# Plain products for the first 512 inner features of each MLP, PSUM banks kept through all stages, pools re-ordered

## The chip, the cores and the metric

The kernel runs on one core of a Trainium2 chip. The metric is the device time of one execution in microseconds (us). The kernel before was timed three times: 2895.0, 2896.69 and 2899.65 us; the median, 2896.69 us, is the time that the change is compared with.

## The reference

One sequence of 1024 tokens with 1024 features goes through an HGRN2 mixer, a squared-ReLU MLP, a multi-head latent attention (MLA) with its shared keys and values, a second MLP and a final norm, all in float32. What the change touches is the MLP and the norms around it:

```python
def rmsnorm(x, gain):
    y = x * lax.rsqrt(jnp.mean(x * x, axis=-1, keepdims=True) + EPS)
    return y * gain

def sq_relu_mlp(xn, w_up, w_down):           # (1024,1024) @ (1024,4096), (4096,1024)
    return jnp.square(jax.nn.relu(xn @ w_up)) @ w_down

h = x
h = h + hgrn2_mixer(rmsnorm(h, hgrn_norm[0]), ...)
h = h + sq_relu_mlp(rmsnorm(h, mlp_norm[0]), mlp_w_up[0], mlp_w_down[0])      # MLP 0
k_nope, k_rope, v = shared_mla_kv(h, kv_in_norm, ...)
h = h + mla_mixer(rmsnorm(h, mla_norm[0]), ..., k_nope, k_rope, v)
h = h + sq_relu_mlp(rmsnorm(h, mlp_norm[1]), mlp_w_up[1], mlp_w_down[1])      # MLP 1
out = rmsnorm(h, final_norm)
```

## The kernel before

The residual stream stays on chip as `hT`, features on partitions, in two halves of 512 tokens (u = 0, 1); the program's rows call it `res`. Every float32 product is done in three matmuls: each operand is split into a high part (a cast to fp32r, on ScalarE, `wh`, `xn`, `hh`) and a low part (the difference, on VectorE or GpSimd, `wl`, `xn`, `hl`), and high x high, high x low and low x high are added in PSUM. A matmul has 512 columns.

**Stages.** HGRN2 mixer (to about 672 us of the profile), MLP 0 (to 1372), MLA (to 2187), MLP 1 (to the end). Each stage opens its own pools of on-chip memory and of PSUM banks: one bank `nb` and three banks `mm` in a mixer, eight banks `ps` in an MLP.

**An MLP** handles its 4096 inner features in eight blocks of 512. A block goes up (two calls of `up`, each for 256 inner features) and down (one call of `down`). Both use the Strassen-Winograd scheme: the operands are cut in 2x2 quarters, and seven products of sums stand for the eight products of quarters. The four quarters of the normed input are B11, B21 (token half 0; the two halves of the 1024 features) and B12, B22 (token half 1). The scheme also needs the sums T1 to T4, made once per MLP on VectorE (`combine` and the low part in `halves`, L529) and ScalarE (the cast in `halves`, L572), in 128x1024 pieces; the 4096-column buffers `fr` and `dn` hold the normed input meanwhile, and later the inner features and the weights of the way down. A product is 12 matmuls (L612); an `up` has 7, so 84 matmuls, a block's two 168, and its `down` (L745) 168.

**The start of an MLP** is `up_first`: both calls of the first block together, product by product. It starts with `inverse(0)` (squares, their sum over features, a matmul with ones (L557), logarithm and exponential, one Newton step) and `normed` (L566) for token half 0, then the products with B11 and B21; the others need T1 to T4, and so both halves of the tokens, `inverse(1)` too. In MLP 1, `finish.turn` also transposes the residual on TensorE (L1159) while the products run.

**The order on the engines** is that of a scheduler which follows the order of the program and its priorities: within `tc.high_priority(offset=n)` an instruction is placed as if it stood n instructions earlier. Each engine works off its own instructions in that fixed order, and waits at each for what it needs.

**In `up`**, the first product's bank x is copied to `fr` by ScalarE (L691) before the third product adds onto x; ScalarE also casts the weights (L602) and the hidden features of the way down (L730). **In `down`** each group of four banks collects 128-row pieces of the output, and VectorE adds them to the residual (L752). In the last block GpSimd also scales and splits the first weights of the next stage (L136, L145, L146, L879 to L882), and the MLA's start splits the residual (L100 on ScalarE, L101 on VectorE) and takes its norm (L484, L486). The scratch of the last `down` lies in the slot `xl0` of a pool for the whole kernel.

Of the kernel before, what the change touches and what calls it, by code (L numbers as in the profile page):

```python
# [17 lines left out]
P = 128  # L18
# [37 lines left out]
def build(nc, tc, a):  # L56
# [8 lines left out]
    pers = ctx.enter_context(tc.tile_pool(name="pers", bufs=1))  # L65
    cur = {}

    @contextmanager
    def common(stage):

        with tc.tile_pool(name=f"w_{stage}", bufs=1, reuse_waits="tile") as w, \
                tc.tile_pool(name=f"n_{stage}", bufs=1, reuse_waits="tile") as n, \
                tc.tile_pool(name=f"o_{stage}", bufs=1, reuse_waits="tile") as o, \
                tc.tile_pool(name=f"one_{stage}", bufs=1, space=PSUM, reuse_waits="tile") as one, \
                tc.tile_pool(name=f"b_{stage}", bufs=1, space=PSUM, reuse_waits="tile") as b:
            cur.update(w=w, n=n, o=o, one=one, b=b)
            yield
            cur.clear()
# [74 lines left out]
    def nbank():  # L153
        return cur["one"].tile([P, 512], F32, tag="nb", name=name("nb"), bufs=1)

    def bank():
        return cur["b"].tile([P, 512], F32, tag="mm", name=name("mm"), bufs=3)
# [347 lines left out]
    def mlp(layer, gain, finish):  # L505
# [5 lines left out]
        with ExitStack() as pools:  # L511
            mt, mu, mw, mf, mh, mp = (pools.enter_context(tc.tile_pool(name=f"mlp{n}{layer}", bufs=1,
                                                                       reuse_waits="tile")) for n in "tuwfhp")
# [23 lines left out]
            for key in ("T2", "T3", "T4"):  # L537
                X[key] = tuple(mt.tile([P, 4, 512], F32R, name=f"{key}{e}") for e in "hl")
            fr = mf.tile([P, 4096], F32, name="fr")
            dn = mf.tile([P, 4096], F32, name="dn")  # L540
            f = {}
            for i, t in enumerate((fr, dn)):
                v = t.rearrange("p (q k t) -> p q k t", q=2, k=4)
                f[i, 0], f[i, 1] = v[:, 0], v[:, 1]
# [4 lines left out]
            def inverse(u):  # L549
# [6 lines left out]
                ps = pbank()  # L556
# [33 lines left out]
            with tc.high_priority(offset=1000):  # L590
# [5 lines left out]
                if finish is not None:  # L596
                    finish.turn(0, pbank)
# [25 lines left out]
            def up_first(A, C):  # L623

                two = range(2)
                w = [parts(G, A[e][0, 0]) for e in two]
                x = [pbank() for _ in two]
                for e in two:
                    product(x[e], w[e], "B11", True, True)
                w = [parts(G, A[e][0, 1]) for e in two]  # L630
                y = [pbank() for _ in two]
                for e in two:
                    product(y[e], w[e], "B21", True, True)
                inverse(1)
                normed(0, 1)
                combine(V, f[0, 1], f[0, 1], f[0, 0])
                halves(V, "T1", f[0, 1])
                normed(1, 1)
                if finish is not None:
                    finish.turn(1, pbank)  # L640
                halves(V, "B22", f[1, 1])
                for e in two:
                    sub(G, A[e][1, 0], A[e][1, 0], A[e][1, 1], ALU.add)
                w = [parts(G, A[e][1, 0]) for e in two]
                z = [pbank() for _ in two]
                for e in two:
                    product(z[e], w[e], "T1", True, True)
                combine(V, f[1, 1], f[1, 1], f[0, 1])
                combine(V, f[0, 1], f[1, 1], f[0, 0])
                halves(V, "T2", f[1, 1])  # L650
                halves(V, "T3", f[0, 1])
                for e in two:
                    sub(G, A[e][1, 0], A[e][1, 0], A[e][0, 0])
                    sub(G, A[e][0, 1], A[e][0, 1], A[e][1, 0])
# [593 lines left out]
```

## Time and profile before

| what | value |
|---|---|
| median of three runs | 2896.69 us |
| the profiled execution's own time | 2896.47 us |
| its span in the trace | 2894.7 us |
| TensorE busy | 2674.8 us (92%), 13141 matmuls |
| VectorE, ScalarE, GpSimd busy | 1850.2, 1195.3, 1348.8 us |
| mean granted TensorE clock | 0.969 of full |

The profiled execution is within 0.3 us of the median, and 1.8 us of it lie outside the span. [...] In the timeline a row is one instruction or a run of like ones: its start, its duration, engine, source line, operation, out<-in, sizes, the count, and in brackets how long the engine had been idle and for what it waited. Matmuls overlap, so a single one's duration is longer than the step from one to the next.

### The profile page before, as it was taken

How to read it: one execution, taken by the hardware profiler on the slowest of the kernel's cores; microseconds unless marked ns; L12 is line 12 of the kernel's file. 1: busy time of each engine (PE TensorE's matmuls, PEld its weight loads, DVE VectorE, ACT ScalarE, POOL GpSimd, SP SyncE). 2: the span in 40 equal slices, each digit the busy share in tenths (PEclk: the TensorE clock that was granted, in tenths of full speed). 3: DMA queues.
4: the chain of work that ended last, by engine and by line, in shares of the span. 5: the costliest groups of instructions: out<-in, count | busy, mean ns of one | idle time of the engine just before them, and what ended most of it. 6: DMA issues, size and time to landing. Idle time of an engine off the chain costs nothing.

```text
span 2894.7 us, 35239 instructions
## 1 busy us (share of the span) xinstructions
PE 2674.8 (92%) x13141; PEld 2200.6 (76%) x13141; DVE 1850.2 (64%) x2970; ACT 1195.3 (41%) x2232; POOL 1348.8 (47%) x870
## 2 busy tenths in 40 slices
PE   7999999896899999996989999999996999999997
PEld 5777877785677787785778888888884777877785
DVE  6677667755855555557676666667667755555567
ACT  4222233223444444444354444444443544444445
POOL 3222223353677766767221122122212777767675
PEclk9999999997999999998999999999997899999999
DMA  4111112140211111110111111111100111111111
GB/s 130 40 37 30 30 44 59 52 135 19 66 52 52 51 59 51 59 55 24 53 42 34 28 50 40 36 39 35 48 19 26 58 52 51 59 51 59 59 48 58
DMA packets 184489, 143.99 MB, mean 50 GB/s; under 512 B 12482, under 2 KB 155903, under 8 KB 184319
## 3 DMA queue, kind: packets, MB, share of 16 engines
q1 hardware_dynamic: 184318, 141.75, 16.3%
q8 instruction: 103, 1.69, 0.2%
q14 instruction: 68, 0.55, 0.1%
HBM read 133.33 MB, written 4.19 MB: 48 GB/s over the span
## 4 chain that ended last, share of the span: by engine, by line
PE 67%; DVE 17%; POOL 6%; ACT 6%; issue 2%; DMA 1%; SPq 0%; DVEq 0%; POOLq 0%; ACTq 0%
PE mm L108 21%; PE ps L612 16%; PE ps L745 13%; PE s L1044 5%; PE nb L1077 3%; DVE hl L529 3%; POOL wl L529 2%; PE mm L1084 2%; POOL wu L529 2%; PE x L366 2%; DVE fr L529 2%; DVE res L752 1%; POOL dn L529 1%; ACT wh L602 1%; ACT hh L730 1%
## 5 line engine op out<-in xcount | busy, mean ns | idle before, releaser
L108 PE MATMUL mm<-xn,wh 128*128 128x512 f32 x1728 | 568.5, 403 | 1.5 <-DVE res L445 0.6
L529 POOL TENSOR_TENSOR wl<-dn,wh 128x512 fp32r<-128x512 f32 x224 | 342.1, 1537 | 115.7 <-ACT wh L602 104.0
L108 PEld LDWEIGHTS mm<-xn,wh 128*128 128x128 f32 x1728 | 321.5, 190 | 64.9 <-issue 3.0
L108 PE MATMUL mm<-xn,wl 128*128 128x512 f32 x864 | 347.2, 402 | 0.0
L146 POOL TENSOR_TENSOR wl<-wst,wh 128x1024 fp32r<-128x1024 f32 (+1 forms) x93 | 221.1, 2380 | 242.9 <-ACT wh L143 240.2
L529 POOL TENSOR_TENSOR wl<-wu,wh 128x512 fp32r<-128x512 f32 x156 | 216.5, 1393 | 186.1 <-PE ps L612 110.5
L752 DVE TENSOR_TENSOR res<-res,ps 128x512 f32<-128x512 f32 x448 | 289.6, 681 | 16.1 <-PE ps L745 15.0
L612 PE MATMUL ps<-xn,wh 128*128 128x512 f32 x1024 | 262.5, 399 | 25.2 <-ACT xn L572 16.2
L602 ACT CAST wh<-dn 128x512 fp32r<-128x512 f32 x224 | 135.9, 619 | 313.5 <-PE ps L745 150.1
L612 PEld LDWEIGHTS ps<-xn,wh 128*128 128x128 f32 x1024 | 196.3, 193 | 72.0 <-ACT xn L572 20.4
L529 DVE TENSOR_TENSOR hl<-fr,hh 128x1024 fp32r<-128x1024 f32 x110 | 198.3, 1804 | 78.1 <-ACT hh L730 78.1
L602 ACT CAST wh<-wu 128x512 fp32r<-128x512 f32 x212 | 130.8, 618 | 261.8 <-POOL wu L529 128.9
L529 POOL TENSOR_TENSOR wu<-wu,wu 128x512 f32<-128x512 f32 x120 | 171.7, 1430 | 143.7 <-DVE wl L529 112.7
L1053 POOL TENSOR_SCALAR P<-P,rc 128x128 f32<-128x128 f32 (+1 forms) x64 | 52.7, 824 | 345.3 <-DVE rc L1051 330.9
L745 PE MATMUL ps<-hh,wh 128*128 128x512 f32 x448 | 176.2, 394 | 23.6 <-DVE res L752 20.5
L108 PEld LDWEIGHTS mm<-xn,wl 128*128 128x128 f32 x864 | 164.3, 190 | 31.7 <-issue 0.9
L745 PE MATMUL ps<-wh,hl 128*128 128x512 f32 x448 | 177.2, 396 | 6.4 <-DVE hl L529 4.1
L745 PE MATMUL ps<-hl,wh 128*128 128x512 f32 x448 | 177.8, 397 | 4.9 <-DVE hl L529 4.9
L745 PE MATMUL ps<-wh,hh 128*128 128x512 f32 x448 | 175.6, 393 | 4.6 <-ACT hh L730 3.2
L529 POOL TENSOR_TENSOR dn<-dn 128x1024 f32<-128x1024 f32 x64 | 167.4, 2615 | 24.3 <-DMA dn<-mlp_w_down 14.6
L745 PE MATMUL ps<-hh,wl 128*128 128x512 f32 x448 | 176.6, 394 | 0.5 <-POOL wl L529 0.5
L745 PE MATMUL ps<-wl,hh 128*128 128x512 f32 x448 | 175.9, 393 | 0.0
(293 smaller groups left out, 6101.3 us busy)
## 6 DMA issues: line engine op xcount, KB each, us to landing
dn<-mlp_w_down SPq DMA_DIRECT2D x64, 512.0 KB, 3.8
wu<-mlp_w_up SPq DMA_DIRECT2D x122, 256.0 KB, 2.8
wst<-hgrn_w_o SPq DMA_DIRECT2D x16, 512.0 KB, 3.9
wst<-mla_w_o SPq DMA_DIRECT2D x16, 512.0 KB, 3.8
wst<-hgrn_w_q SPq DMA_DIRECT2D x10, 512.0 KB, 3.9
wst<-hgrn_w_i SPq DMA_DIRECT2D x10, 512.0 KB, 3.8
wst<-hgrn_w_g SPq DMA_DIRECT2D x10, 512.0 KB, 3.9
wst<-hgrn_w_f SPq DMA_DIRECT2D x9, 512.0 KB, 3.8
```

The lines of the kernel that those rows point to most:

```text
L108: T.matmul(ps, l, r, start=i == 0, stop=i == n - 1)
L146: G.tensor_tensor(out=wl[:, cs], in0=st[:, cs], in1=wh[:, cs].bitcast(F32), op=ALU.subtract)
L366: T.matmul(ps[:m, c * 64:(c + 1) * 64], k[:, c * P:c * P + m], bl(q[:, c * P:(c + 1) * P], h, 1), start=True, stop=True)
L529: eng.tensor_tensor(out=out, in0=x, in1=y, op=op)
L602: S.copy(out=wh, in_=x)
L612: T.matmul(bank, l[:, k, :], r[:, k, :], start=start and n == 0, stop=n == 11, skip_group_check=not start)
L745: T.matmul(banks[i], l, r, start=start and k == 0 and n == 0, stop=k == 1 and n == 2, skip_group_check=not start)
L752: V.tensor_tensor(out=o, in0=o, in1=banks[i], op=ALU.add)
L1044: T.matmul(ps[:, at + u * HALF:at + u * HALF + w_], l, r, start=e == 0, stop=e == len(terms) - 1)
L1053: G.tensor_scalar(out=pt[:, :n], in0=pt[:, :n], scalar1=rc, scalar2=1.0, op0=ALU.mult, op1=ALU.mult)
L1077: T.matmul(dst, l, r[:, cols_], start=j == 0 and e == 0, stop=j == 2 * g + 1 and e == 2)
L1084: T.transpose(tr[:, n * P:(n + 1) * P], Ps[e][:, j * P:(j + 1) * P], ident)
```

## The change

- `up_first` becomes `up_plain`: the first block's inner features are computed in 16 plain products (four tiles of 128 inner features x two halves of the input features x two halves of the tokens), each of 12 matmuls. The eight products of token half 0 come first. After them in the program, but 300 instructions ahead by priority, stand `inverse(1)`, `normed` and the split of B12 and B22; then come the products of token half 1. T1 to T4 are made after that in the program's order and are first used by the second block. The slot of T4 holds B12 until then. `fr` now holds token half 0 and `dn` half 1. Results go from PSUM through the ReLU straight to `fr`.
- The PSUM pools `one` (bank `nb`) and `three` (banks `mm`) are opened once for the kernel. An MLP has four banks `ps` of its own; `banks_of(s)` gives those (s = 0) or the three `mm` and `nb` (s = 1), and `up` and `down` alternate between the sets.
- Pools are opened in another order: `o` before `n` in a mixer, and t, d, f, u, w, h, p in an MLP, `dn` in a pool of its own.
- In `up`, the copy L691 (now L688) is issued ahead of the parts of the fourth weight (`tc.issue_after`).
- The last `down` of MLP 0 has its scratch in the slot of T4's low part, not in `xl0`. At the MLA's start the raised priority is gone, and both halves are split before the two norms.

```diff
-            mt, mu, mw, mf, mh, mp = (...  for n in "tuwfhp")
+            mt, md, mf, mu, mw, mh, mp = (... for n in "tdfuwhp")
-            def pbank():
-                return pp.tile([P, 512], F32, tag="ps", name=name("ps"), bufs=8)
+            def banks_of(s, n=4):
+                if s == 0:
+                    return [pp.tile([P, 512], F32, tag="ps", name=name("ps"), bufs=4) for _ in range(n)]
+                return [bank() for _ in range(min(n, 3))] + [nbank() for _ in range(n - 3)]
...
-            def up_first(A, C):
...
+            def up_plain(A, C):
+                tiles = [(1, 0), (1, 1), (0, 0), (0, 1)]
+                acc, w = {}, {}
+                def step(t, u, k):
+                    e, i = t
+                    if (t, k) not in w:
+                        w[t, k] = parts(G, A[e][i, k])
+                    product(acc[t, u], w[t, k], ("B11", "B21", "B12", "B22")[2 * u + k], k == 0, k == 1)
+                def out(t, u):
+                    relu(C[t[0]][t[1], u], acc[t, u])
+                for t in tiles:
+                    acc[t, 0], = banks_of(0, 1)
+                    for k in range(2):
+                        step(t, 0, k)
+                with tc.high_priority(offset=300):
+                    inverse(1)
+                    normed(0, 1)
+                    normed(1, 1)
+                    if finish is not None:
+                        finish.turn(1, banks_of)
+                    halves(V, "B12", f[0, 1])
+                    halves(V, "B22", f[1, 1])
+                for t, b in zip(tiles[::-1], banks_of(1)):
+                    acc[t, 1] = b
+                for k in range(2):
+                    for n, t in enumerate(tiles[::-1]):
+                        if n > 1:
+                            w.pop((t, k))
+                        step(t, 1, k)
...
-                S.copy(out=C[0, 0], in_=x)
+                kept = S.copy(out=C[0, 0], in_=x)
...
-                s3 = parts(G, A[1, 0])
+                with tc.issue_after(kept.ins):
+                    s3 = parts(G, A[1, 0])
...
-                scr = pers.tile([P, 4096], F32, tag="xl0", name=name("scr"))
+                if finish is None:
+                    scr = mt.tile([P, 2048], F32, tag="T4l", name=name("scr"))
+                else:
+                    scr = pers.tile([P, 4096], F32, tag="xl0", name=name("scr"))
...
-        with tc.high_priority(offset=1000):
-            for u in range(2):
...
-                inv[u] = inv_rms(ntmp, lambda k: hT[u][:, k, :], KT)
+        for u in range(2):
+            inv[u] = inv_rms(ntmp, lambda k: hT[u][:, k, :], KT)
```

**TensorE at the start of MLP 0.** `ps` and `mm` are banks, `xn` is a part of B11 to B22 or T1, `wh` and `wl` the weight's parts, L557 (now L562) the sum of squares, `hh` its input. Before, at the end of the four products that need token half 0 alone:

```order
L612 MATMUL ps_5738<-xn_5627,wh_5733 128x512 x4
L612 MATMUL ps_5738<-xn_5629,wh_5733 128x512 x4
L612 MATMUL ps_5738<-xn_5627,wl_5734 128x512 x4
L557 MATMUL ps_5778<-hh_5639,onef 128x512
L612 MATMUL ps_5814<-xn_5628,wh_5806 128x512 x4
L612 MATMUL ps_5814<-xn_5630,wh_5806 128x512 x4
```

On the same engine now, from the last transposes of the mixer on:

```order
L443 MATMUL x_5592<-ident,xr_5590 128x128 x4
L617 MATMUL ps_5696<-xn_5628,wh_5697 128x512 x4
L617 MATMUL ps_5696<-xn_5630,wh_5697 128x512 x4
L617 MATMUL ps_5696<-xn_5628,wl_5698 128x512 x2
L562 MATMUL nb_5843<-hh_5640,onef 128x512
L617 MATMUL ps_5696<-xn_5628,wl_5698 128x512 x2
L617 MATMUL ps_5696<-xn_5628,wh_5713 128x512 x4
```

The matmul of `inverse(1)` moved from behind 48 matmuls into the first product, and behind it there are 182 plain matmuls, of which 86 still need token half 0 alone. That of `inverse(0)` no longer stands here; it moved up into the mixer's output projections, with 14 matmuls of its group and five whole groups of 24 behind it.

**ScalarE in the second `up` of a block.** `hh` is the high part of hidden features for the way down, `fr<-ps` the copy of bank x, `wh` a weight's high part. Before:

```order
L602 CAST wh_6524<-wu_6475 128x512
L620 ACTIVATE fr<-ps_6349 128x512
L617 ACTIVATE fr<-fr 128x512
L602 CAST wh_6545<-wu_6475 128x512
L730 CAST hh_6632<-fr 128x1024
L691 COPY fr<-ps_6494 128x512
L730 CAST hh_6644<-fr 128x1024
```

The same place now:

```order
L607 CAST wh_6525<-wu_6476 128x512
L625 ACTIVATE fr<-mm_6350 128x512
L622 ACTIVATE fr<-fr 128x512
L728 CAST hh_6633<-fr 128x1024
L688 COPY fr<-ps_6495 128x512
L607 CAST wh_6546<-wu_6476 128x512
L728 CAST hh_6645<-fr 128x1024
```

The cast of the fourth weight moved from ahead of the first hidden cast to behind the copy.

**GpSimd in the last `down` of MLP 0.** `wl<-dn` are low parts of this `down`'s weights, `wst` the next stage's. Before:

```order
L529 TENSOR_TENSOR wl_10192<-dn,wh_10191 128x512
L136 TENSOR_TENSOR wst_10573<-wst_10573,vecs 128x1024
L145 TENSOR_SCALAR wh_10576<-wst_10573 128x1024
L136 TENSOR_TENSOR wst_10606<-wst_10606,vecs 128x1024
L529 TENSOR_TENSOR wl_10196<-dn,wh_10195 128x512
L146 TENSOR_TENSOR wl_10577<-wst_10573,wh_10576 128x1024
L529 TENSOR_TENSOR dn<-dn 128x1024
```

The same place now:

```order
L532 TENSOR_TENSOR wl_10193<-dn,wh_10192 128x512
L532 TENSOR_TENSOR wl_10197<-dn,wh_10196 128x512
L532 TENSOR_TENSOR dn<-dn 128x1024
L532 TENSOR_TENSOR wl_10240<-dn,wh_10239 128x512
L532 TENSOR_TENSOR wl_10244<-dn,wh_10243 128x512
L136 TENSOR_TENSOR wst_10569<-wst_10569,vecs 128x1024
L145 TENSOR_SCALAR wh_10572<-wst_10569 128x1024
L136 TENSOR_TENSOR wst_10602<-wst_10602,vecs 128x1024
```

The next stage's work moved behind three more low parts and one sum of the way down; as many instructions stand there in all.

## Rows read from the trace of the kernel before

**Rows 1.** The page, part 1: busy us, share of the span, instructions.
```profile
PE 2674.8 (92%) x13141; PEld 2200.6 (76%) x13141; DVE 1850.2 (64%) x2970; ACT 1195.3 (41%) x2232; POOL 1348.8 (47%) x870
```

**Rows 2.** Busy time by stretches: length, each engine's busy us, clock, DMA.
```profile
672.61:797.63 125.02, 92.04 (x343) 69.30 (x342) 102.53 (x102) 56.17 (x83) 67.21 (x39) 0.82 0.14 44
797.63:876.32 78.69, 76.76 (x337) 62.91 (x337) 44.35 (x50) 36.12 (x58) 56.32 (x37) 1.00 0.18 54
1307.82:1373.79 65.97, 43.85 (x171) 34.02 (x169) 54.06 (x59) 25.73 (x43) 48.00 (x26) 0.82 0.10 26
2186.88:2323.11 136.23, 101.50 (x406) 80.07 (x405) 106.82 (x110) 61.71 (x94) 74.69 (x44) 0.82 0.15 49
```

**Rows 3.** TensorE's waits, whole run: us in total, times, longest.
```profile
PE ps L745 <- DVE res L752: 21.8, 4, 18.4
PE ps L612 <- ACT fr L691: 19.5, 14, 1.5
PE ps L612 <- ACT xn L572: 16.2, 3, 8.7
PE ps L557 <- DVE hh L555: 15.6, 2, 9.4
```

**Rows 4.** The chain of waits: start, length, engine and line.
```profile
797.63 19.05 PE ps L612 x84
```

**Rows 5.** TensorE's timeline at the start of MLP 0.
```profile
672.61 1.02 PE L557 MATMUL ps<-hh,onef 128*128 128x512 f32 x2
680.45 3.97 PE L612 MATMUL ps<-xn,wh 128*128 128x512 f32 x8 [6.82 <-ACT xn L572]
754.08 1.39 PE L745 MATMUL ps<-hh,wh 128*128 128x512 f32 x4 [3.18 <-ACT hh L730]
```

**Rows 6.** VectorE's timeline around it.
```profile
640.52 2.11 DVE L555 TENSOR_TENSOR hh<-hh 128x512 f32<-128x512 f32 x1 [0.70 <-ACT hh L553]
673.42 0.69 DVE L445 TENSOR_TENSOR res<-res,mm 128x512 f32<-128x512 f32 x1 [5.24 <-ACT res L444]
677.90 2.74 DVE L566 SCALAR_TENSOR_TENSOR fr<-res,vecs,hl 128x512 f32<-128x512 f32 x4
```

**Rows 7.** VectorE and GpSimd while T2 and T3 are made in MLP 1.
```profile
2248.28 2.35 DVE L529 TENSOR_TENSOR T2l<-dn,T2h 128x1024 fp32r<-128x1024 f32 x2
2250.59 4.51 DVE L529 TENSOR_TENSOR T3l<-fr,T3h 128x1024 fp32r<-128x1024 f32 x2
...
2247.28 4.50 POOL L529 TENSOR_TENSOR wl<-wu,wh 128x512 fp32r<-128x512 f32 x1 [28.63 <-PE ps L612]
2267.62 1.28 POOL L529 TENSOR_TENSOR wl<-hl,wh 128x512 fp32r<-128x512 f32 x1
2268.85 2.38 POOL L529 TENSOR_TENSOR dn<-dn 128x1024 f32<-128x1024 f32 x1
```

**Rows 8.** DMA issues, 700 to 760 us: count, size, us to landing.
```profile
dn<-mlp_w_down SPq DMA_DIRECT2D x4, 512.0 KB, 5.4
```

**Rows 9.** TensorE's timeline at the start of MLP 1.
```profile
2186.88 1.02 PE L557 MATMUL ps<-hh,onef 128*128 128x512 f32 x2
2187.74 3.66 PE L1159 MATMUL ps<-ident,res 128*128 128x128 f32 x32
2199.42 1.22 PE L612 MATMUL ps<-xn,wh 128*128 128x512 f32 x2 [8.03 <-ACT res L1162]
```

**Rows 10.** Timelines of three engines in a block's second `up`.
```profile
818.50 1.86 DVE L529 TENSOR_TENSOR fr<-fr 128x1024 f32<-128x1024 f32 x1 [3.22 <-ACT fr L617]
...
821.53 0.62 ACT L602 CAST wh<-wu 128x512 fp32r<-128x512 f32 x1 [3.07 <-POOL wu L529]
822.06 1.04 ACT L730 CAST hh<-fr 128x1024 fp32r<-128x1024 f32 x1
823.00 0.58 ACT L691 COPY fr<-ps 128x512 f32<-128x512 f32 x1
...
823.63 1.20 PE L612 MATMUL ps<-T2h,wh 128*128 128x512 f32 x4 [1.53 <-ACT fr L691]
```

**Rows 11.** Timelines of TensorE and VectorE in MLP 0's last `down`.
```profile
1344.59 0.77 PE L745 MATMUL ps<-hh,wh 128*128 128x512 f32 x1 [18.42 <-DVE res L752]
1373.79 0.73 PE L108 MATMUL mm<-xn,wh 128*128 128x512 f32 x2 [0.43 <-DVE res L752]
...
1329.40 5.80 DVE L101 TENSOR_TENSOR xn<-res,xn 128x512 fp32r<-128x512 f32 x3 [8.07 <-ACT xn L100]
```

More of the change, by code (lines that the diff above doesn't have):

```diff
@@ L65, in build @@
     pers = ctx.enter_context(tc.tile_pool(name="pers", bufs=1))
+    one = ctx.enter_context(tc.tile_pool(name="one", bufs=1, space=PSUM))
+    three = ctx.enter_context(tc.tile_pool(name="three", bufs=1, space=PSUM))
     cur = {}
@@ L636, in up_first @@
                 combine(V, f[0, 1], f[0, 1], f[0, 0])
                 halves(V, "T1", f[0, 1])
[L638 to L647, printed above, removed]
@@ L648, in up_first @@
                 combine(V, f[1, 1], f[1, 1], f[0, 1])
                 combine(V, f[0, 1], f[1, 1], f[0, 0])
+                for t in tiles[2:]:
+                    out(t, 0)
+                halves(V, "T3", f[0, 1])
+                combine(V, f[1, 0], f[1, 0], f[1, 1])
                 halves(V, "T2", f[1, 1])
[L651 to L654, printed above, removed]
@@ L655, in up_first @@
-                w = [parts(G, A[e][0, 1]) for e in two]
-                z2 = [pbank() for _ in two]
-                for e in two:
-                    product(z2[e], w[e], "B22", True, True)
-                w = [parts(G, A[e][1, 0]) for e in two]
-                for e in two:
-                    sub(G, A[e][1, 0], A[e][1, 1], A[e][1, 0])
-                    S.copy(out=C[e][0, 0], in_=x[e])
-                    V.tensor_tensor(out=C[e][0, 0], in0=C[e][0, 0], in1=y[e], op=ALU.add)
-                    S.copy(out=C[e][1, 1], in_=z[e])
-                    product(x[e], w[e], "T2", False, True)
@@ L737, in times @@
                 if start:
-                    banks = [pbank() for _ in range(4)]
+                    banks = banks_of(banks)
                 for k in range(2):
@@ L755, in times, with down @@
                 return banks
-            def down(A, last):
+            def down(A, s, last):
                 A11, A12, A21, A22 = A
@@ L792, in down @@
                 w2, h2 = weights(A12), hidden(B21)
-                q = times(None, w1, h1, True, [(0, 0)])
+                q = times(s, w1, h1, True, [(0, 0)])
                 sub(V, t2, B22, B12)
                 w6, h6 = weights(A11), hidden(t2)
-                times(None, w2, h2, True, [(0, 0)], finish and (lambda i: finish.squares(0, i, 0)))
+                times(1 - s, w2, h2, True, [(0, 0)], finish and (lambda i: finish.squares(0, i, 0)))
                 sub(G, A12, A12, A11)
@@ L807, in down @@
                 w3, h3 = weights(A12), hidden(B22)
-                p = times(None, w5, h5, True, [(1, 1)], finish and (lambda i: finish.squares(1, i, 1)))
+                p = times(1 - s, w5, h5, True, [(1, 1)], finish and (lambda i: finish.squares(1, i, 1)))
                 times(p, w3, h3, False, [(1, 0)], finish and (lambda i: finish.ended(1, i, 0)))
@@ L822, in mlp @@
                     A1 = load_up(2 * fb + 1)
-                    up(A1, outs(1))
+                    up(A1, outs(1), st)
+                    st = 1 - st
                 if not last:
                     A0 = load_up(2 * fb + 2)
-                down(down_A, last)
+                down(down_A, st, last)
     mlp(0, R_MLP0, None)
@@ L1152, in build, with turn @@
     class Finish:
-        def turn(self, u, pbank):
+        def turn(self, u, banks_of):
             for dh in range(2):
-                banks = [pbank() for _ in range(4)]
+                banks = banks_of(u)
                 for c in range(4):
```

89 lines of the change are left out of this document (35 added, 54 removed).

## The prediction, made before the changed kernel ran

> **What bounds the kernel now.** I read the page's busy times first: TensorE works 2674.8 us, 92% of the span, and no other engine more than 64% [rows 1]. So time can be won only where TensorE waits or runs at the low clock, and every matmul added costs its full step. The chain of waits gives that step: 84 matmuls in 19.05 us, 0.2268 us each [rows 4]. Then I cut the span into stretches. A block in the middle of an MLP (168 matmuls up, 168 down, 336 x 0.2268 = 76.2 us) takes 78.7 us at clock 1.00; the first block of MLP 0 takes 125.0 us for nearly as many matmuls, that of MLP 1 136.2 us with 64 short matmuls more, and the last `down` of MLP 0 66.0 us where 168 x 0.2268 = 38.1 would do. All three stand at clock 0.82 [rows 2]: TensorE waited, and the granted clock fell with it. The list of waits names what is waited for: parts of the normed input (16.2 us), the squares under L557 (15.6 us), VectorE's L752 in a last `down` (21.8 us, 18.4 of it one wait) and, 14 times up to 1.5 us, the copy L691 (19.5 us) [rows 3]. The change touches each of these four.
>
> The sum is made against the profiled execution's 2896.47 us (span 2894.7, 1.8 outside it), which is 0.2 us under the median; I treat them as one.
>
> **Added matmuls.** 16 plain products are 192 matmuls, seven in two calls are 168: 24 x 0.2268 = 5.4 us per MLP. They are counted inside the next two steps.
>
> **Start of MLP 0, now 672.6 to 797.6.** The sum for token half 0 moves into the mixer, five groups and 14 matmuls before its end. A group there goes with one add of VectorE, 0.69 + 5.24 = 5.93 us [rows 6]; so TensorE arrives at L562 near 672.6 - 5 x 5.93 - 14 x 0.2268 = 639.8. VectorE's squares are ready at 640.52 + 2.11 = 642.6 [rows 6]: a wait of about 3 us, and I take 4 with a little slow clock (bounds 0 and 6) instead of the 6.82 us wait and the two L557 after 672.6 [rows 5]. Products then start near 677; with 1.5 us for the wait at the other sum, 192 x 0.2268 = 43.5 us end near 721.6.
>
> What the first `down` waits for is VectorE. Its weights land in `dn`, which now holds the normed half 1 until T2's low part, the last piece that reads it there, is made. VectorE's queue up to that piece: the last residual add, over at 674.1 [rows 6] and 4 later for the wait at L562; its square, 1.6, to 679.7; from that half's L562 to its first `normed` 5.3, as from 672.61 [rows 5] to 677.90 [rows 6] now, to 685, eight `normed` at 0.69 (2.74 for four [rows 6]) to 690.5, and some 18 pieces of 128x1024 at 2.35 / 2 = 1.18 us [rows 7], to 711.7. Beside GpSimd such a piece has taken 4.51 / 2 = 2.26 us [rows 7]: bounds for this are 0 and 18 x 1.08 = 19.4 us; I take 6, since GpSimd has about five instructions there. VectorE is free near 717.5; the weights land 5.4 us after their issue [rows 8]; GpSimd's sum of them takes 2.38 us [rows 7], cast and handoffs 1. First L743 near 726.5, some 5 us after the last product; 2 us more for a lowered clock and 38.1 us of `down` end near 767. Against 797.6 that is **-30 us** (bounds -17, all pieces contended, to -36, none).
>
> **Start of MLP 1, now 2186.9 to 2323.1.** The transposes and normed pieces still stand before the first product at 2199.4 [rows 9], which I leave at 2200. Token half 0: 96 x 0.2268 = 21.8, with 32 transposes at 3.66 / 32 = 0.114 [rows 9] 3.7 more, and 4 for waits and clock: 2229.5. Half 1: 2251.3. VectorE's T chain starts when half 1 is normed, about 2229: 14 pieces x 1.18 = 16.5, and 5.5 for contention, 2251; then weights 5.4, sum 2.38, cast 1: first `down` near 2260, 2 for the clock and 38.1: 2300. **-23 us** (bounds -13, all 14 contended, and -29, where the products alone decide).
>
> **The kept copy.** In the second `up` ScalarE cast a weight at 821.53 and hidden features at 822.06 (1.04 us) before the copy at 823.00, and TensorE took its bank 1.53 us late, at 823.63 [rows 10]. VectorE's piece before it ends at 818.50 + 1.86 = 820.36; with the weight's cast behind the copy, the hidden cast runs from 820.4 to 821.4, the copy to 822.0, and TensorE wants the bank at 822.1. All 14 waits go: 14 x 1.39 = **-19 us** (bounds -19.5 and 0). The fourth weight comes 0.5 us later; the product between hides it (12 matmuls, 2.7 us).
>
> **The last `down` of MLP 0 and the MLA's start.** TensorE waits 18.42 us at L745 for L752 [rows 11], because the splits of the next stage (L101, which itself waits 8.07 us for ScalarE [rows 11]) are queued ahead of it on VectorE. Without the raised priority and the scratch in `xl0`, L750 stands ahead of L101, and three more low parts stand ahead of the next stage's weights on GpSimd. What is late next is GpSimd: its work in the stretch is 48.0 us of 66.0 [rows 2], so the next stage's first matmul comes at about 50 us instead of 66: **-15 us** (bounds -6, if VectorE beside it stretches that work by a quarter, and -22, all of L752's waits). The MLA's norm comes later; about 65 matmuls, 14.7 us, run before a bank depends on it, so I put it at 0 (bounds -8, VectorE's 8.07 us wait, and +3, four steps of 0.69 in its chain). Keeping PSUM pools open and alternating two sets of four costs nothing as long as a set is free again in time; see the last rival.
>
> Sum: -30 - 23 - 19 - 15 = -87 us, from 2896.5: **about 2810 us**.
>
> **Rivals.**
> *Operands late.* TensorE has its input early, but T1 to T4 and the weights behind them on VectorE take 2.26 us a piece throughout. For it: the pair at 2250.59 took 4.51 [rows 7]. Against: the pairs before it took 2.35. About +14 at each start: -59, 2837 us. Chance 0.15.
> *The copy's wait is only replaced.* GpSimd's sum, the cast and the low part of the fourth weight now come after the copy, and TensorE waits there instead, 14 times. The product of slack (2.7 us) against 1.28 for a low part and 0.62 for a cast speaks against it. -68, 2828 us. Chance 0.12.
> *GpSimd starved.* While VectorE runs its pieces back to back, GpSimd's low part of a weight took 4.50 us at 2247.28, where one took 1.28 at 2267.62 [rows 7]. Plain products need eight new weight pieces and each is used at once; four pairs per MLP each 1.5 us late give +12: 2822 us. Chance 0.10.
> [...]
> *Four banks are too few (slower).* With sets of four instead of eight, a group starts only when VectorE has emptied the set used before. If TensorE waits there for four adds of 0.69 and a handoff, 3.1 us, three times in each of 14 blocks, that is 130 us: 2940 us. It decides from 87 / (14 x 3.1) = 2 such waits in a block. Against it: between two uses of a set lies at least a group of 24 matmuls, 5.4 us, and the adds take 2.8. Chance 0.04.
> Sides of the forecast: the last `down` keeps its wait, 2825 us, or all ends fall well, under 2786.
>
> **How the numbers follow.** The forecast 2810 has 0.59 with its bounds; the rivals 0.15, 0.12, 0.10 and 0.04 as above. Less than 0.2% (6 us) is what a measurement cannot tell from no change; only the last rival, or several shortfalls at once, end there or beyond: faster 0.94, same 0.02, slower 0.04. The bounds added up at the good end give -36 - 29 - 19.5 - 22 - 8 = -114; they will not all come, and I stop at 2786. At the poor end -17 - 13 - 0 - 6 + 3 = -33, 2863; I stop at 2852, which takes in the first three rivals.
>
> **What would show it.** First product near 677 in MLP 0, a short wait at L562 in the mixer at 639 to 643; a gap of some 5 us before the first L743 of MLP 0 and 9 of MLP 1; no wait for L688 in the list, and middle blocks of about 77.3 us; in the last `down` of MLP 0 no long wait for L750, but a wait for GpSimd's weights, and L108 some 50 us after its start. It is wrong if a middle block is longer than 78.7 us, if the first L743 comes after 745 or 2280, or if the MLA's start gives back what the last `down` won.

## The result, and the profile after

The changed kernel takes 2856.01 us (median; 2851.03 to 2859.48) against 2896.7: ratio 0.9857, interval 0.984 to 0.9874. It is faster by 41 us where 87 were forecast, and 4 us above the upper end of the range. The profiled execution's span is 2853.9 us, 40.8 below the one before. Matmul starts in the two traces cut it into stretches that add up (here and below, the `up` of a block means its two calls together, 168 matmuls):

| stretch (from, to) | before | after | change | forecast |
|---|---|---|---|---|
| to the first product of MLP 0 | 680.5 | 684.5 | +4.0 | -3.5 |
| its first block up, to the first L743 | 73.6 | 56.0 | -17.7 | -24 |
| its first `down` | 43.4 | 42.2 | -1.2 | -3 |
| 7 `up` and 6 `down` between | 510.3 | 506.8 | -3.6 | -9.5 |
| last `down`, to the MLA's first L108 | 66.0 | 55.9 | -10.1 | -15 |
| MLA, to the first product of MLP 1 | 825.6 | 828.4 | +2.8 | 0 |
| first block of MLP 1, up and down | 123.5 | 112.3 | -11.2 | -23 |
| 7 `up` and 6 `down` between | 510.7 | 505.6 | -5.1 | -9.5 |
| last `down` and final norm | 61.1 | 62.3 | +1.2 | 0 |

The runs further down show how far such a figure wanders where nothing was edited: the last `down` of MLP 0 took 55.9 to 59.2 us, and MLP 1's first `down`, 50.0 in the changed kernel's trace, 47.0 to 48.8 in six runs that leave all of MLP 1's start as it is. So changes of 2 or 3 us in one of these lines say nothing, and 1 to 3 us of MLP 1's first block are of that kind.

The same stretches by busy time, in the columns of [rows 2]:

```profile
684.49:782.66 98.17, 86.60 (x366) 69.06 (x364) 79.26 (x74) 44.08 (x64) 60.55 (x30) 0.97 0.18 57
782.66:860.54 77.88, 76.68 (x337) 62.84 (x336) 43.94 (x50) 36.27 (x57) 57.19 (x37) 1.00 0.18 55
1289.42:1345.28 55.86, 43.84 (x170) 33.64 (x169) 52.04 (x48) 24.21 (x39) 49.63 (x26) 0.91 0.12 32
2173.69:2285.99 112.30, 96.43 (x394) 75.28 (x395) 84.68 (x85) 48.58 (x72) 60.03 (x30) 0.93 0.16 50
```

The first block of MLP 0 has lost most of its low clock (0.82 to 0.97), as has that of MLP 1 (0.82 to 0.93); in the last `down` the clock is 0.91 and GpSimd is busy 49.6 of 55.9 us. A middle block fell only from 78.69 to 77.88.

TensorE's waits over the whole run, to be set against [rows 3]:

```profile
PE mm L743 <- DVE hl L532: 15.6, 12, 3.4
PE ps L743 <- DVE hl L532: 12.3, 10, 1.8
PE mm L617 <- POOL wl L532: 11.2, 2, 6.5
PE nb L562 <- DVE hh L560: 7.6, 4, 5.6
PE ps L743 <- POOL wl L532: 6.7, 4, 4.4
PE mm L743 <- DVE res L750: 4.8, 2, 3.8
PE mm L108 <- DVE res L445: 3.7, 3, 3.1
```

The copy (19.5 us) and the normed input (16.2 us) are gone from the list. New are two long waits for weight parts `wl` that GpSimd makes, and waits inside the mixer. The waits for low parts `hl` in `down` are not new but three times as long in total, 27.9 us; before, they were:

```profile
PE ps L745 <- DVE hl L529: 9.1, 18, 2.1
```

**In the mixer**, TensorE's timeline (a group of 24 matmuls and 4 transposes takes 5.93 us there):

```profile
642.16 2.07 PE L562 MATMUL nb<-hh,onef 128*128 128x512 f32 x2 [5.62 <-DVE hh L560]
663.83 1.19 PE L108 MATMUL mm<-xn,wh 128*128 128x512 f32 x2 [3.15 <-DVE res L445]
```

and VectorE's over the same time:

```profile
641.36 0.74 DVE L560 TENSOR_TENSOR hh<-hh 128x512 f32<-128x512 f32 x1
648.51 5.54 DVE L571 SCALAR_TENSOR_TENSOR fr<-res,vecs,hl 128x512 f32<-128x512 f32 x4
663.01 0.68 DVE L445 TENSOR_TENSOR res<-res,mm 128x512 f32<-128x512 f32 x1
```

The wait for the squares was 5.62 us. Then the whole norm of half 0 (from 648.51) stood ahead of the residual add at 663.01, which frees a bank, and TensorE waited another 3.15. Between 630 and the mixer's end the clock was 0.87 where it had been 1.00. The mixer ended 11.9 us later.

**At both MLP starts** one GpSimd instruction took about seven times the 1.27 and 1.28 us of the next one. VectorE, GpSimd and TensorE in MLP 0:

```profile
713.40 2.35 DVE L532 TENSOR_TENSOR dn<-dn,fr 128x1024 f32<-128x1024 f32 x2
715.67 2.35 DVE L532 TENSOR_TENSOR fr<-fr,dn 128x1024 f32<-128x1024 f32 x2
717.95 1.21 DVE L532 TENSOR_TENSOR T2l<-dn,T2h 128x1024 fp32r<-128x1024 f32 x1
719.08 2.35 DVE L532 TENSOR_TENSOR T3l<-dn,T3h 128x1024 fp32r<-128x1024 f32 x2
721.35 1.21 DVE L532 TENSOR_TENSOR T2l<-dn,T2h 128x1024 fp32r<-128x1024 f32 x1
...
715.15 8.53 POOL L532 TENSOR_TENSOR wl<-hh,wh 128x512 fp32r<-128x512 f32 x1 [8.44 <-ACT wh L607]
723.65 1.27 POOL L532 TENSOR_TENSOR wl<-wu,wh 128x512 fp32r<-128x512 f32 x1
...
723.74 1.65 PE L617 MATMUL mm<-T4h,wl 128*128 128x512 f32 x3 [6.47 <-POOL wl L532]
```

and in MLP 1:

```profile
2216.71 1.21 DVE L532 TENSOR_TENSOR T2l<-dn,T2h 128x1024 fp32r<-128x1024 f32 x1
2221.72 2.67 DVE L532 TENSOR_TENSOR T3l<-dn,T3h 128x1024 fp32r<-128x1024 f32 x2 [3.79 <-ACT T3h L577]
...
2209.98 9.06 POOL L532 TENSOR_TENSOR wl<-hh,wh 128x512 fp32r<-128x512 f32 x1 [12.70 <-PE mm L617]
...
2219.08 0.62 ACT L607 CAST wh<-hl 128x512 fp32r<-128x512 f32 x1 [4.58 <-POOL wl L532]
...
2219.10 1.20 PE L617 MATMUL mm<-T4h,wl 128*128 128x512 f32 x3 [4.73 <-POOL wl L532]
```

VectorE falls idle at 721.35 + 1.21 = 722.56 and at 2217.92; GpSimd's instruction ends at 723.68 and 2219.04, both times 1.12 us later. That is near the 1.27 us of the next low part, at 723.65; how much of its work it did before VectorE fell idle, the rows do not show. In MLP 1 the delay went on from engine to engine: ScalarE waited 4.58 us for that low part, cast T3 late, and VectorE stood idle for 3.79 us.

Earlier in the same chain it went another way:

```profile
699.85 3.45 DVE L532 TENSOR_TENSOR T4l<-dn,T4h 128x1024 fp32r<-128x1024 f32 x2
...
700.28 1.93 POOL L532 TENSOR_TENSOR wl<-wu,wh 128x512 fp32r<-128x512 f32 x1 [2.23 <-ACT wh L607]
```

Here GpSimd needed only 1.93 us, and VectorE's two pieces took 3.45 us instead of 2.35. The same holds for two more pieces at 705.50 (3.44 us), and the eight `normed` before them took 7.35 us instead of 5.5 (2.74 for four [rows 6]): VectorE lost about 4 us in MLP 0. Why both engines' instructions took a little longer there, and at 715.15 GpSimd's alone and by 7 us, no run shows.

**In a middle `down`** (from 898.77), TensorE's start, then GpSimd, ScalarE, VectorE, TensorE:

```profile
898.77 0.39 PE L743 MATMUL ps<-hh,wh 128*128 128x512 f32 x1
...
903.01 2.41 POOL L532 TENSOR_TENSOR dn<-dn 128x1024 f32<-128x1024 f32 x1
...
905.46 1.14 ACT L607 CAST wh<-dn 128x512 fp32r<-128x512 f32 x2 [5.22 <-POOL dn L532]
906.50 1.04 ACT L728 CAST hh<-fr 128x1024 fp32r<-128x1024 f32 x1
...
907.58 2.19 DVE L532 TENSOR_TENSOR hl<-fr,hh 128x1024 fp32r<-128x1024 f32 x1 [2.48 <-ACT hh L728]
914.33 2.39 DVE L532 TENSOR_TENSOR hl<-fr,hh 128x1024 fp32r<-128x1024 f32 x1
...
916.78 0.50 PE L743 MATMUL mm<-hl,wh 128*128 128x512 f32 x1 [1.20 <-DVE hl L532]
```

and the same `down` before:

```profile
916.06 0.39 PE L745 MATMUL ps<-hh,wh 128*128 128x512 f32 x1
...
918.44 3.27 POOL L529 TENSOR_TENSOR dn<-dn 128x1024 f32<-128x1024 f32 x1
```

GpSimd's sum now ends 6.65 us after the `down`'s first matmul, before 5.65. Counted from the block's first product, TensorE comes 1.67 us sooner and the sum only 0.67; the 1.0 us between is what a `down` lost. ScalarE waits for it with two weight casts; the hidden cast stands behind them, and VectorE's queue behind that runs without a gap from 907.58 to the low part that TensorE misses at 916.78.

### The profile page after: what moved, and what is told of

It is laid out like the page before. It is cut to its first block, busy times and chain, and to the rows that moved or that the text cites. A ratio compares the mean times of both kernels' runs of the same rounds, so it can differ in the third digit from the quotient of the medians.

```text
span 2853.9 us, 35266 instructions
## 1 busy us (share of the span) xinstructions
PE 2677.4 (94%) x13189; PEld 2203.1 (77%) x13189; DVE 1845.8 (65%) x2958; ACT 1191.8 (42%) x2220; POOL 1343.9 (47%) x850
## 4 chain that ended last, share of the span: by engine, by line
PE 65%; DVE 18%; ACT 6%; POOL 5%; issue 4%; DMA 2%; SPq 0%; DVEq 0%; POOLq 0%; ACTq 0%
PE mm L108 20%; PE mm L617 8%; PE ps L617 8%; PE ps L743 6%; PE s L1046 5%; PE mm L743 5%; PE nb L1079 3%; DVE hl L532 3%; POOL wl L532 2%; PE mm L1086 2%; DVE fr L532 2%; DVE res L750 2%; PE x L366 2%; PE nb L743 2%; POOL dn L532 1%
## 5 line engine op out<-in xcount | busy, mean ns | idle before, releaser
L108 PE MATMUL mm<-xn,wh 128*128 128x512 f32 x1728 | 573.3, 406 | 4.7 <-DVE res L445 3.7
L532 POOL TENSOR_TENSOR wl<-dn,wh 128x512 fp32r<-128x512 f32 x224 | 363.3, 1637 | 98.8 <-ACT wh L607 95.0
L108 PEld LDWEIGHTS mm<-xn,wh 128*128 128x128 f32 x1728 | 323.2, 191 | 69.1 <-issue 7.2
L108 PE MATMUL mm<-xn,wl 128*128 128x512 f32 x864 | 349.1, 404 | 0.0
L108 PEld LDWEIGHTS mm<-xn,wl 128*128 128x128 f32 x864 | 165.4, 191 | 33.2 <-issue 2.1
L532 DVE TENSOR_TENSOR fr<-fr 128x1024 f32<-128x1024 f32 x58 | 115.2, 1986 | 68.7 <-ACT fr L622 67.8
L1052 ACT ACTIVATE P<-s,mx 128x384 f32<-128x384 f32 (+7 forms) x128 | 95.0, 742 | 139.4 <-DVE mx L1050 120.3
L617 PE MATMUL ps<-xn,wh 128*128 128x512 f32 x576 | 146.1, 395 | 0.2 <-ACT res L1164 0.2
L750 DVE TENSOR_TENSOR res<-res,ps 128x512 f32<-128x512 f32 x216 | 138.5, 680 | 12.0 <-PE ps L743 11.7
L1079 PE MATMUL nb<-h,xn 128*128 128x256 f32 (+1 forms) x640 | 136.9, 292 | 0.1
L145 POOL TENSOR_SCALAR wh<-wst 128x1024 fp32r<-128x1024 f32 (+2 forms) x57 | 65.9, 1160 | 137.7 <-PE mm L108 121.1
L617 PEld LDWEIGHTS ps<-xn,wh 128*128 128x128 f32 x576 | 108.8, 190 | 23.5 <-ACT res L1164 0.7
L100 ACT CAST h<-mm 128x512 fp32r<-128x512 f32 (+1 forms) x160 | 82.8, 546 | 101.6 <-PE mm L1086 101.4
L728 ACT CAST hh<-fr 128x1024 fp32r<-128x1024 f32 x110 | 115.2, 1047 | 24.1 <-DVE fr L532 23.9
```

What stands on the lines that cost most here:

```text
L100: S.copy(out=out_h, in_=src)
L108: T.matmul(ps, l, r, start=i == 0, stop=i == n - 1)
L532: eng.tensor_tensor(out=out, in0=x, in1=y, op=op)
L617: T.matmul(bank, l[:, k, :], r[:, k, :], start=start and n == 0, stop=n == 11, skip_group_check=not start)
L728: S.copy(out=hh, in_=Bq)
L750: V.tensor_tensor(out=o, in0=o, in1=banks[i], op=ALU.add)
```

## The experiments

All times are medians of four executions, ratios to the kernel before on the same chip. Stretches are from one profiled execution each. The first seven runs undo or alter one thing of the changed kernel. The kernel before took 2894.3 to 2897.1 us in the three rounds of these runs (2896.7 beside the changed kernel), so a difference in us between runs of different rounds carries up to 3 us of that; where it matters, the difference of the ratios is given too.

| run | us | ratio, interval |
|---|---|---|
| a_lows | 2845.31 | 0.9831, 0.9816 to 0.9845 |
| b_late | 2863.91 | 0.9897, 0.9882 to 0.9912 |
| b_mid170 | 2839.13 | 0.9801, 0.9787 to 0.9816 |
| c_copy | 2861.96 | 0.9886, 0.9869 to 0.9902 |
| f_hid2 | 2839.77 | 0.9809, 0.9795 to 0.9824 |
| d_prio | 2854.2 | 0.985, 0.9833 to 0.9866 |
| e_scr | 2850.91 | 0.9841, 0.9826 to 0.9855 |
| de_both | 2854.68 | 0.9857, 0.9837 to 0.9876 |
| best | 2824.77 | 0.9751, 0.9736 to 0.9765 |
| best2 | 2820.89 | 0.9739, 0.9722 to 0.9756 |

**a_lows: what does GpSimd's long low part at each start cost?**

```diff
-                        w[t, k] = parts(G, A[e][i, k])
+                        w[t, k] = parts(V if u else G, A[e][i, k])
```

> The four low parts of weights that GpSimd makes during VectorE's T chain at each MLP start are made by VectorE instead (4 x 0.69 us more on VectorE per MLP). Theory: GpSimd is shut out by VectorE's back-to-back pieces (its low part took 8.53 and 9.06 us and ended 1.1 us after VectorE fell idle), and TensorE's waits of 6.47 and 4.73 us come from that; they go, the first block of MLP 0 (98.2 us) takes about 91, that of MLP 1 (112.3) about 103, total about 2840. Rival: VectorE's chain itself is the limit, since the first weights of the way down need T2's low part; the first L743 then comes as late as now or 3 us later, total 2856 to 2862.

11 us faster by the medians, 7.5 by the ratios, whose intervals overlap slightly. Both waits for `wl` in `up` are gone; the first block of MLP 0 takes 95.8 us (98.2), that of MLP 1 104.6 (112.3). VectorE took on eight low parts, and T2's last one in MLP 0 ended at 722.63 (722.56), in a run whose mixer ended 1.75 us sooner. In MLP 1 most of the theory's 9 us came; but six runs that leave that start alone have 109.0 to 111.4, so the edit itself is worth 4 to 7 there. In MLP 0 a third came, since another wait stood behind. GpSimd and TensorE of this run:

```profile
728.49 2.40 POOL L532 TENSOR_TENSOR dn<-dn 128x1024 f32<-128x1024 f32 x1 [23.50 <-DMA dn<-mlp_w_down]
...
735.09 0.79 PE L743 MATMUL ps<-hh,wh 128*128 128x512 f32 x1 [4.31 <-ACT hh L728]
```

The four loads of the `down`'s weights go out from 718.05 on, the last at 722.66, when T2's low parts are made, which lands 5.8 us later, at 728.5; then come the sum, the weight casts and, behind those on ScalarE, the hidden cast. So the rival's mechanism is there too, as the second limit.

**b_late and b_mid170: what is the early sum worth, and where should it stand?** b_late gives the sum a bank of the MLP, b_mid170 lowers its priority.

```diff
-                ps = nbank()                                            # b_late
+                ps = nbank() if u or finish is not None else banks_of(0, 1)[0]
...
-            with tc.high_priority(offset=1000):                         # b_mid170
+            with tc.high_priority(offset=1000 if finish is not None else 170):
```

> The sum for token half 0 of MLP 0 uses a bank of the MLP, so that its matmul stands behind the mixer again. Theory: the early sum lengthened the mixer by 11.9 us (waits of 5.6 and 3.1 us and low clock) and gains less at the first product: without it the first product comes at about 680.5 instead of 684.5, but VectorE's norm and T chain start later, so the first L743 stays near 740: total 2853 to 2860. Rival: the early sum is a clear gain, as predicted (first product 4 us before the 680.5 of the kernel before): without it the first block is later by 8 or more, total 2864 or above.

> MLP 0's sum for token half 0 is placed with a lower priority: its matmul stands 41 rows later among TensorE's rows, still inside the mixer. Theory: the mixer is 11.9 us longer because TensorE reaches that matmul 5.0 to 5.6 us before VectorE has the squares, and VectorE's norm then holds up a residual add (3.1 us); two groups (11.9 us) later the first wait is gone and the first product comes at 676 to 680 instead of 684.5, total 2848 to 2852. Rival: the norm itself then comes too late for the first product, and the gain is spent there: first product at 684 or later, total 2856 or above.

In b_late the first product came at 678.2, 6.3 us sooner, but the first L743 at 746.6 and the next block at 791.8, 9.1 us later than in the changed kernel. My theory (2853 to 2860) fell, and the rival's 2864 was measured. The 9.1 us are not the late norm alone, though: GpSimd's low part took still longer, 12.88 us, and TensorE waited 9.01 us for it.

```profile
708.79 12.88 POOL L532 TENSOR_TENSOR wl<-hh,wh 128x512 fp32r<-128x512 f32 x1 [11.56 <-PE mm L617]
...
721.73 2.07 PE L617 MATMUL mm<-T4h,wl 128*128 128x512 f32 x4 [9.01 <-POOL wl L532]
```

No run has b_late together with a_lows, so the two shares are not separated. In b_mid170, with the sum and the norm two groups later in the mixer, the stretch up to the first product (first the changed kernel's, then this run's, in the columns of [rows 2]) is:

```profile
630.00:684.49 54.49, 45.73 (x192) 36.17 (x190) 34.01 (x36) 19.02 (x30) 21.96 (x12) 0.87 0.18 52
```

```profile
630.00:671.77 41.77, 41.77 (x196) 34.10 (x195) 30.74 (x36) 19.34 (x31) 21.53 (x12) 1.00 0.28 75
```

TensorE has no gap there (busy 41.77 of 41.77 us), the clock is 1.00, and products follow the mixer at once. The sum's matmul no longer waits:

```profile
647.25 1.02 PE L562 MATMUL nb<-hh,onef 128*128 128x512 f32 x2
```

The first product is 12.7 us sooner, more than the theory's 4.5 to 8.5: 8.8 us are the two waits, 4.0 the matmuls' own time (45.73 us for 41.77) at the lower clock (0.87). The time is 17 us lower, below the theory's 2848; the rest lies mostly in MLP 1's first block (109.0 for 112.3), which this edit does not touch. Both waits in the mixer and its low clock thus came from the place of this sum and norm, which stood too early.

**c_copy: the copy's wait, put back.**

```diff
-                with tc.issue_after(kept.ins):
-                    s3 = parts(G, A[1, 0])
+                s3 = parts(G, A[1, 0])
```

> The fourth weight is no longer held back behind the copy; all else as in the changed kernel. Theory: the order on ScalarE alone took the 1.53 us wait out of each up and put 1.0 us into each down (GpSimd's weights are not faster): up goes back to 39.9 and down to 38.65 us, total 2856 + 8.7 = 2865. Rival: the two sets of banks took part; then up stays near 38.2 or down at 39.65.

`up` went back to 39.92 us and `down` to 38.7; the two middle stretches to 510.7 and 510.8. The waits are the old ones, eight in one set of banks and six in the other:

```profile
PE ps L617 <- ACT fr L688: 10.4, 8, 1.5
PE mm L617 <- ACT fr L688: 9.2, 6, 1.5
```

So holding back the fourth weight behind the copy is the whole of this step, and the bank sets have no share. Its price is 9.1 us in the two middle stretches here, 8.65 between the kernel before and the changed one; the median rose by only 6 (theory: 9), in part because MLP 1's first block took 110.2 us and not 112.3.

**f_hid2: the hidden cast ahead of the weight casts.**

```diff
-                    w3, h3 = weights(A11), hidden(B22)
+                    h3 = hidden(B22)
+                    with tc.issue_after(casts[-1]):   # hidden()'s cast
+                        w3 = weights(A11)
```

> In down the cast of the hidden features for the third product stands ahead of the two casts of its weights on ScalarE. Theory: the 1.2 us wait of each middle down ends a chain GpSimd sum, weight casts, hidden cast, VectorE's queue, low part; with the hidden cast ahead it goes: down 39.65 to about 38.6 us, 12 to 14 times, total 2842 to 2845. Rival: GpSimd's low parts of the weights are as late as the hidden features; the wait turns into one for them, total 2853 to 2858.

16 us faster by the medians, 14 by the ratios, and so below the theory's 2842; middle `down`s take 38.9 us instead of 39.65 (theory: 38.6), a middle block 77.1. The two middle stretches fell by 4.8 us each, MLP 1's first `down` from 50.0 to 44.9, 2 to 4 us under the runs that leave it alone. The chain through GpSimd's sum and ScalarE's queue was what took back the copy's gain. The waits for `hl` fell from 27.9 us to 7.5; in their place stand 12 waits of about 0.5 us for the weight casts, which now come second:

```profile
PE mm L746 <- ACT wh L607: 3.2, 6, 0.5
PE ps L746 <- ACT wh L607: 3.1, 6, 0.6
```

**d_prio, e_scr, de_both: who cured the last `down`?** Each puts back one edit, the third both.

```diff
-        for u in range(2):
-            xh, xl = ...split...
-        for u in range(2):
-            inv[u] = inv_rms(...)
+        with tc.high_priority(offset=1000):           # d_prio, de_both
+            for u in range(2):
+                xh, xl = ...split...
+                inv[u] = inv_rms(...)
...
-                if finish is None:
-                    scr = mt.tile([P, 2048], F32, tag="T4l", name=name("scr"))
+                scr = pers.tile([P, 4096], F32, tag="xl0", name=name("scr"))   # e_scr, de_both
```

> The raised priority at the MLA's start is put back (splits, then the norm of each half); the scratch stays in T4's slot, so that GpSimd's order is that of the changed kernel. Theory: the last down of MLP 0 got its 10 us from the slot of the scratch, which set GpSimd's order; then the stretch from its first L743 to the first L108 stays within 1 us of 55.9, total 2854 to 2859. Rival: the priority did it, by putting L101 ahead of L750 on VectorE: 61 to 66 us, total 2861 to 2866.

> The scratch of MLP 0's last down goes back to the slot xl0; the priority stays away. GpSimd then has the next stage's weights ahead of three low parts and a sum of this down. Theory (slot): the stretch grows from 55.9 to 62 to 66 us, total 2862 to 2866, with L101 or L743 waiting for xl0's reader. Rival (priority): it stays within 1 us of 55.9.

> Both back in the last down of MLP 0: the raised priority at the MLA's start and the scratch in xl0; banks and pools as in the changed kernel. Undone singly they left the stretch from its first L743 to the first L108 at 60.0 and 57.3 us (55.8 to 59.2 in the runs that touch neither). Theory: either alone is enough, since L101 must be ahead of L750 and the scratch must wait for L101's reader for the 18 us wait to arise; with both back the stretch takes 64 to 68 us, total 2862 to 2868. Rival: the kept banks removed the wait; the stretch stays at 56 to 60, total 2850 to 2856.

The stretch took 60.0, 57.3 and 59.8 us; the changed kernel has 55.9, runs that touch neither edit up to 59.2. By the stretch all three theories missed, and of the rivals only that of de_both came. So neither edit, nor both, carries the 10 us. The long wait itself is another matter. With the scratch alone put back (e_scr) much of it returns, and so does VectorE's wait ahead of it:

```profile
1311.02 1.60 DVE L101 TENSOR_TENSOR xn<-res,xn 128x512 fp32r<-128x512 f32 x1 [8.08 <-ACT xn L100]
...
1319.78 0.77 PE L743 MATMUL mm<-hh,wh 128*128 128x512 f32 x1 [11.99 <-DVE res L750]
```

The changed kernel waits 3.75 us there, d_prio 2.72: the slot of the scratch brings 8 of the 18.4 us, the priority none. It hardly shows in the stretch, since TensorE's waits for GpSimd's `wl` fall from 6.3 us to 1.3 with it. All waits of the stretch come to 22.2 us before, 12.1 in the changed kernel, 15.7 in e_scr and 15.5 in de_both. In de_both the old picture, on TensorE and VectorE, beside [rows 11]:

```profile
1318.19 0.77 PE L743 MATMUL mm<-hh,wh 128*128 128x512 f32 x1 [11.97 <-DVE res L750]
...
1309.44 5.79 DVE L101 TENSOR_TENSOR xn<-res,xn 128x512 fp32r<-128x512 f32 x3 [8.09 <-ACT xn L100]
```

L101 again stands ahead of L750 and waits 8.09 us for ScalarE, but TensorE's wait is 11.97 instead of 18.42, as with the scratch alone. The other thing ahead of L752 before, the norm's L484, is no longer there. What removes it and these last 6.4 us, the kept banks or the order of the pools, was not separated and stays open.

**best and best2: the edits that won, together.** best is a_lows, f_hid2 and b_mid170 in one; best2 also makes T2 before T3 and loads the quarters of the first sum first.

```diff
+                halves(V, "T2", f[1, 1])
+                combine(V, f[1, 0], f[1, 0], f[1, 1])
                 halves(V, "T3", f[0, 1])
-                combine(V, f[1, 0], f[1, 0], f[1, 1])
-                halves(V, "T2", f[1, 1])
...
-                for i, (d, k) in enumerate(((0, 0), (0, 1), (1, 0), (1, 1))):
+                for i, d, k in ((2, 1, 0), (3, 1, 1), (0, 0, 0), (1, 0, 1)):
```

> The four low parts on VectorE, the hidden cast ahead of the weight casts, and the later sum for token half 0, together. Theory: the three act at different places (first blocks, middle downs, mixer's end) and add up, less 3 to 5 us where the first and second both took time from the first down: 2856 - 11 - 16 - 5 + 4 = about 2828, 2823 to 2833. Rival: the first down is bound by its weights' landing (8.7 us from issue to landing in the run with the low parts on VectorE), so that what comes earlier in the mixer is lost again there: 2834 to 2840.

> As the version with three edits, and in each MLP's start T2's parts are made before T3's, and of the way down's weights the two quarters that the first sum needs are loaded first. Theory: the first down is now bound by its weights, whose four loads are issued behind T2's low part and take 8.7 us to land; two of them issued about 3 us earlier bring the first down 3 to 5 us forward in each MLP: 2824.8 - 8 = about 2817, 2815 to 2820. Rival: the hidden features, behind the same VectorE queue, are as late: 2822 to 2826.

The total, 2825, lies in the theory's range, but by luck: the sum had 5 us for b_mid170, which brought 17, and 3 to 5 us of overlap. Singly the three runs won 11, 16 and 17 us, 44 in all; together they won 31. Most of the missing 13 is MLP 1's first block: it fell by 7.7, 5.7 and 3.3 us in the single runs and by 6.8 in best, so what could be won there, and what had wandered, was counted three times. best2's median is 4 us lower still, between theory and rival and with intervals that overlap. (The 8.7 us to landing in its expectation are counted from the second of four loads; a load takes 3.9 to 5.8 in a_lows.) Its first `up`s are 3.0 and 1.8 us shorter, and TensorE's wait at the first matmul of MLP 0's first `down` fell from 4.73 us (best) to 1.73 (best2):

```profile
726.27 0.79 PE L746 MATMUL ps<-hh,wh 128*128 128x512 f32 x1 [4.73 <-ACT hh L730]
```

```profile
721.55 0.49 PE L746 MATMUL ps<-hh,wh 128*128 128x512 f32 x1 [1.73 <-ACT hh L730]
```

best2 is 35 us faster than the changed kernel and 76 faster than the one before.

## Why the prediction was wrong, point by point

The direction and every place named were right, and none of the signs of being wrong that the prediction lists came (a middle block of 77.9 us, first L743 at 740.5 and 2236.0). The sum was off by 46 us: 7.5 before the first product, 8 in MLP 0's first block, 12 in MLP 1's, 10 in the blocks between, 5 in the last `down`, 4 in the stages put at 0. What failed is of one kind: each step was priced at the wait that it removes, and what the next engine's queue does with the time was put at little or nothing.

- **The early sum (start of MLP 0).** "I take 4 with a little slow clock" for L562's wait in the mixer. The mixer grew by 11.9 us. I priced the wait at the matmul (5.62 us in place of 3, since TensorE came 3 us earlier than reckoned) and forgot what VectorE does next: the norm of half 0 goes ahead of the residual adds that free the mixer's banks, which cost 3.15 us more; most of the rest is the low clock (0.87 from 630 us on, 1.00 in b_mid170). b_mid170 shows that nothing of it is needed: with the matmul two groups later the mixer's end and the forecast's first product (677) are beaten by 5 us. My theory after the result, that the early sum wins nothing, missed too (b_late), though how much it wins there is mixed with GpSimd's longer wait.
- **Contention at the starts.** I charged 6 us of slower pieces to VectorE in MLP 0 and gave "GpSimd starved" 12 us and a chance of 0.10. Both came: VectorE lost about 4 us, and then, while its pieces ran without a gap at 1.2 us each, one low part on GpSimd took 8.53 and 9.06 us, and TensorE waited 6.47 and 4.73 us for it. What GpSimd makes afterwards is late too, as is ScalarE's queue behind it, most of all in MLP 1 (a wait of 4.58 us). a_lows prices this at 7 to 11 us for both starts, near the rival's 12. The rival's 1.5 us for each of four pairs was my estimate, and no run shows it: in the changed kernel one low part per start took some 7.3 and 7.8 us more than 1.28, beside six whole VectorE pieces, and the next three took 1.27 to 1.30 us in MLP 0 and 1.28 to 1.88 in MLP 1.
- **What the first `down` waits for.** Path and landing were right: 5.8 us from the last issue to the landing (a_lows) for 5.4 [rows 8]. But VectorE's chain ends at 722.56 instead of 717.5: half 1's first `normed` comes at 692.58 for the 685 reckoned, behind the longer mixer, which outweighs the smaller loss to slower pieces. And from the sum to the first L743 it is 4.2 us instead of 1 in a_lows: the hidden cast stands behind ReLUs and weight casts on ScalarE. The first L743 of a_lows is late by these two, 735.1 for 726.5. In the changed kernel itself the gap of 5 us did not come at all: TensorE, late through GpSimd's low part, went straight from its products to the first L743 at 740.47.
- **The first `down` itself.** I let it run at 38.1 us and 2 for the clock. In MLP 0 it took 42.2, in MLP 1 50.0, and there lies most of MLP 1's miss: its first L743 came 62.3 us after the first product, where 60 were forecast. Waits of 7.1 us for weights and hidden parts, which I had put at nothing, and the low clock (0.93, TensorE busy 42.85 us for the 38.1), 2.8 us more than the 2 charged, make up the 10. Without GpSimd's late low part this `down` took 44.1 us (a_lows), with the hidden cast first 44.9 (f_hid2), and 1 to 3 us are wander.
- **The kept copy.** "All 14 waits go": they did, 1.67 us per `up` of most blocks, 21.9 us in all where 19 were forecast. About 1.0 us per `down` came back, 13 us in the 12 middle ones, a term that the sum doesn't have. The rival "only replaced" had the right shape and the wrong place: I looked for the next wait at the next weight, within the `up`; it stood one call later, where GpSimd's sum, which came only 0.67 us sooner, feeds ScalarE, VectorE and TensorE in turn (f_hid2). I had written that a block would take 77.3 us without asking what paces GpSimd (56.3 us busy of 78.7 [rows 2]).
- **The last `down`.** -10 for -15. GpSimd is the next limit as said (waits for `wl` of 0.90, 4.36 and 1.06 us), but its 49.6 us of work took 55.9: one wait of 3.75 for L750 and two for `hl` are left. Of the reasons I gave, the priority removed nothing that stands out, and the scratch's slot 8 us of the long wait, 5 of which GpSimd's waits took back; what removed the rest stays open (e_scr, de_both).
- **Two slips in the sum.** "About +14 at each start" in the rival of late operands fits MLP 0 only: for MLP 1 its own numbers give 15.1 - 5.5 = 9.6 us, and 2833 for the time. And the bound of -29 in MLP 1 is that of a chain without contention; the products alone would give -32.
- **Right:** the kept banks at no cost: no product or `down` of a middle block waits for L750, and the rival of four banks is out. The MLA's start gave nothing back that stands out: its stretch took 828.4 us, 826.5 to 830.1 in the other runs.

## What to carry to other kernels

When a wait goes, follow the next engine's own pace through the following stage, not only the next instruction: an instruction that does not come as much sooner can hand the time back one call later (here GpSimd's sum came 0.67 us sooner for TensorE's 1.67, and 1.0 was lost). When a matmul is moved up into another stage, count what its input's engine will do right after it, and who waits for that engine there; a group or two later can be worth more than the earliest place (here 12.7 us at the first product, in b_mid170). Gains of edits that meet in the same stretch do not add up (here 44 us singly, 31 together). Keep low parts that TensorE needs next off GpSimd while VectorE runs a gapless chain (here one such part took 8.53 and 9.06 us, and TensorE waited 6.47 and 4.73 for it).

## What the runs showed of the hardware that was not expected

A GpSimd instruction took far longer beside a gapless run of VectorE instructions: where the low parts right after it took 1.27 and 1.28 us, it took 8.53 and 9.06 us, and 12.88 in b_late, and in the changed kernel it ended 1.12 us after VectorE fell idle both times. In c_copy and f_hid2, which leave these low parts on GpSimd, TensorE's two waits for them come to 10.7 us, the longest 6.5 (11.2 and 6.5 in the changed kernel). One of the same form took 1.30 us at 729.82, after the chain. VectorE's pieces in that stretch took 1.2 us each, as at 703.23 (2.35 for two). Nor is it always so: at 700.28 and 705.21 GpSimd's instructions took 1.93 and 1.51 us, and VectorE's pairs of pieces beside them 3.45 and 3.44 us instead of 2.35. What decides between the two was not found.
